# Expert weights in two buffer sets, gate columns computed in the feed-forward, and the residual's transposes inside expert 0

## The chip, the cores and the metric

The kernel runs on one core of a Trainium2 chip. The metric is the device time of one execution in microseconds (us), the median of several runs. PE is the matrix engine (PEld its weight loads), DVE the vector engine, ACT the scalar engine, POOL the GpSimd engine, and SP the engine whose queue starts most of the large DMA transfers.

## The reference

Two layers work on 512 latent tokens of width 1024 (and 256 context tokens). Each layer is an RMS norm with modulation, a projection into three token mixers (gated DeltaNet, attention, short convolution), an output projection, a gated residual, a second modulated norm and a channel mixer. In layer 0 the channel mixer is a dense feed-forward of width 2816, in layer 1 a mixture of 8 experts, of which each token uses two. The part that matters here is layer 1 from the output projection on:

```python
m_lat = (s_lat @ w_mod[l] + b_mod[l])[:, None, :]
sh1, sc1, g1, sh2, sc2, g2 = jnp.split(m_lat, 6, axis=-1)
...
x = x + g1 * out_l                              # out_l = cat @ w_out
hl2 = modulate(rmsnorm(x, norm2[l]), sh2, sc2)
x = x + g2 * channel_mixer(hl2, ...)            # layer 1: moe_swiglu
...
probs = jax.nn.softmax((h @ router).astype(F32), axis=-1)
top_p, top_i = lax.top_k(probs, TOP_K)
...
out = out + comb[..., e:e + 1] * swiglu(h, wg[e], wu[e], wd[e])
```

All is float32 at the ends. The gate row g2 of layer 1 stands in columns 5120 to 6143 of `s_lat @ w_mod[1]`, that is in column groups 10 and 11 of 512 columns each.

## The kernel before

**Weights.** Every weight tile is 128 x 1024 float32 (512 KB). `weight` loads it into a `raw` buffer through SP's queue (L196), ACT rounds it to `hi` (L207), and DVE subtracts to `lo` (L208); a product is then three matmuls (hi by hi, hi by lo, lo by hi). The pools that hold raw, hi and lo are opened by `weights`, and each tile waits until its buffer is free.

**Order of the work.** The program is written once as straight code, and a scheduler puts each engine's instructions into that engine's own order, by dependences and by when it takes each of them to be ready. Each engine then runs its row in order, so an instruction that waits holds up all behind it. DMA transfers stand in the row of the engine that issues them.

**The output projection of layer 1** (`tail`). The 512 tokens go in two pieces of 256: MID (token tiles 1 and 2) and ENDS (tiles 0 and 3). For each piece and each of eight blocks `m` of 128 output rows there is one `wout` tile and 24 matmuls (L215 to L217) over the eight parts `cat0` to `cat7`; then DVE adds to the residual tile `xr` in place (L730), which ACT's queue has loaded (L700). Raw has 4 buffers there, hi and lo 3. Just ahead, the last scan steps of gated DeltaNet and the last attention tiles run on the same engines (copies `L` and `a_pt` on ACT; `oacc` and `go_r` on DVE are the scan's output and its norm; `cat0` and `cat1` come from them last).

**The second norm.** After each piece, `stats` squares the eight blocks on ACT and DVE in turn, sums them in PE (L341), transposes the sums, takes the reciprocal root on DVE in 12 small steps (`rsq`, L239 to L246), and spreads it by a diagonal tile (`dg`) and a matmul (L357). DVE scales (L739) and ACT adds the shift (L740) to give `hh`. After the second piece, `mod_rows` computes the gate row: 8 `wmod` tiles, 32 matmuls (L265), a copy, a matmul with `sel` (L746) and an addition to `g2row` (L747).

**The mixture of experts** (`moe`). Router matmuls (L898), `lt` copies, four small transposes (L1062), scores `lg` (L1066). `route` picks two experts a token and computes each row's place: `sel`, four running sums `cum` (L1084), matmuls (L1087 to L1089), `pos`, `p0`, the one-hot `eq` (L1096), and from it the row numbers `first` of expert 0's tokens (L1102). The tokens of `hh` are transposed into `tk` (`tokens`) and written to memory by SP (L903); POOL gathers expert 0's rows `xa` and `xb` from there (L1227, L1235), PE transposes them, ACT and DVE split them into `xh` and `xl`. Then the residual `xr` is transposed into `tk` (32 transposes, L231 and L889), the pools of `hh` and `xr` are closed, and raw becomes a pool of 7 buffers in place of 4.

**The experts** (`Expert.run`). Each of the eight has ten steps: five of four gate and up tiles (`wmg`), one of two, and four of down tiles (`wmd`). Step `i` computes while the tiles of step `i+1` are loaded and split. hi and lo have 8 buffers each. Where an expert has more than 128 tokens, extra matmuls stand in a branch on a flag, which every engine reads out of `jobs` (L933, the branches L1267). `gate` and `out` (L1303, L1304) follow each step's matmuls; `gm` is the gated product. `Combine` gathers and adds the results during the last two experts.

## Time and profile before

| | us |
|---|---|
| median of 3 runs | 2132.27 (2132.15 to 2135.34) |
| the profiled execution | 2134.24 |
| its span, first to last instruction | 2132.5 |
| PE busy in the span | 2011.8 (94%) |
| DVE / ACT busy | 1398.4 / 996.0 |
| last matmul of layer 1's output projection starts | at 1499.67 |
| gather of expert 0's rows is issued | at 1528.44 |
| first matmul of expert 0 | at 1542.38 |

The profiled execution took 2.0 us longer than the median of the timed runs and 1.7 us longer than its own span. Times "at" are counted from the start of the span. PE is the engine to follow: stretches in which it is not busy, or in which its granted clock (PEclk, as a share of full speed) is below 1.00, are where time is lost.

### The profile page before, as it was taken

The numbers are of one execution on the slowest core, as the hardware profiler recorded it, in microseconds if no ns is written. First come the engines' busy times: TensorE is split into PE (matmuls) and PEld (weight loads), VectorE is DVE, ScalarE is ACT, GpSimd is POOL, SyncE is SP. The second block draws the span as 40 slices with busy tenths as digits, with TensorE's granted clock in tenths as the row PEclk, the third lists the DMA queues.
The fourth block names the chain that finished last, engine by engine and source line by source line (L and its number), as shares of the span: only waits on it lengthen the run. The fifth ranks groups of instructions, "written<-read, shape, count | busy, mean of one in ns | idle before, by whom it ended". The sixth has DMA issues, their size and how long they took to land. (4 is left out here: it accounts for less than half of the span.)

```text
span 2132.5 us, 33501 instructions
## 1 busy us (share of the span) xinstructions
PE 2011.8 (94%) x12422; PEld 1647.2 (77%) x12422; DVE 1398.4 (66%) x2501; ACT 996.0 (47%) x1748; POOL 229.5 (11%) x276
## 2 busy tenths in 40 slices
PE   6999899989999999999989998999789999999996
PEld 2998766768788888888879886778567777777774
DVE  3858855765896734242367598677576788666777
ACT  3665375543322222222246556654365576645555
POOL 0000222214000000000040004210110000000011
PEclk9999999999999999999999999999899999999998
DMA  6342543152564715131233333034597799667674
GB/s 260 93 134 70 166 163 115 33 172 93 197 207 129 246 42 206 33 102 50 69 123 108 102 102 117 22 117 146 168 327 255 257 353 332 214 222 240 241 277 157
DMA packets 123489, 344.56 MB, mean 162 GB/s; under 512 B 13280, under 2 KB 36816, under 8 KB 123312
## 3 DMA queue, kind: packets, MB, share of 16 engines
q1 hardware_dynamic: 81216, 273.85, 38.3%
q0 software_dynamic: 14608, 47.87, 6.7%
q10 hardware_dynamic: 27488, 20.52, 3.1%
q8 instruction: 106, 1.74, 0.3%
q14 instruction: 71, 0.58, 0.1%
HBM read 306.00 MB, written 36.19 MB: 160 GB/s over the span
## 5 line engine op out<-in xcount | busy, mean ns | idle before, releaser
L207 ACT ACTIVATE hi<-raw 128x1024 fp32r<-128x1024 f32 (+3 forms) x444 | 426.2, 987 | 302.2 <-PE ps L216 230.7
L208 DVE TENSOR_TENSOR lo<-raw,hi 128x1024 fp32r<-128x1024 f32 (+2 forms) x432 | 482.7, 1138 | 85.5 <-ACT hi L207 69.5
L215 PE MATMUL ps<-hh,hi 128*128 128x512 f32 (+1 forms) x1040 | 355.8, 342 | 0.8 <-ACT hi L207 0.8
L217 PE MATMUL ps<-hh,lo 128*128 128x512 f32 (+1 forms) x1040 | 353.9, 340 | 1.7 <-DVE lo L208 1.7
L216 PE MATMUL ps<-hl,hi 128*128 128x512 f32 (+1 forms) x1040 | 354.6, 341 | 0.0
L215 PEld LDWEIGHTS ps<-hh,hi 128*128 128x128 f32 x1040 | 198.2, 191 | 26.7 <-ACT hi L207 3.4
L217 PEld LDWEIGHTS ps<-hh,lo 128*128 128x128 f32 x1040 | 198.1, 190 | 24.2 <-DVE lo L208 2.5
L216 PEld LDWEIGHTS ps<-hl,hi 128*128 128x128 f32 x1040 | 198.3, 191 | 21.2
L223 PE MATMUL ps<-lo,xh 128*128 128x512 f32 (+1 forms) x384 | 150.6, 393 | 10.7 <-DVE lo L208 5.1
L221 PE MATMUL ps<-hi,xh 128*128 128x512 f32 (+1 forms) x384 | 145.9, 380 | 2.0 <-ACT hi L207 1.9
L222 PE MATMUL ps<-hi,xl 128*128 128x512 f32 (+1 forms) x384 | 144.7, 377 | 0.0
L1332 DVE TENSOR_TENSOR sg<-sg,ps 128x512 f32<-128x512 f32 (+1 forms) x44 | 24.4, 554 | 150.7 <-PE ps L217 150.7
L217 PE MATMUL ps<-gh,lo 128*128 128x256 f32 (+1 forms) x352 | 119.2, 338 | 2.8 <-DVE lo L208 2.8
L216 PE MATMUL ps<-gl,hi 128*128 128x256 f32 (+1 forms) x352 | 120.2, 342 | 0.0
L215 PE MATMUL ps<-gh,hi 128*128 128x256 f32 (+1 forms) x352 | 119.2, 339 | 0.0
L223 PEld LDWEIGHTS ps<-lo,xh 128*128 128x128 f32 x384 | 72.4, 189 | 38.7 <-DVE lo L208 16.5
L296 DVE SCALAR_TENSOR_TENSOR macc<-mraw,sT,macc 128x512 f32<-128x512 f32 x126 | 89.4, 749 | 13.7 <-DMA mraw<-wmod 12.8
L221 PE MATMUL ps<-hi,hh 128*128 128x400 f32 (+2 forms) x272 | 91.7, 338 | 1.3 <-ACT hi L207 1.1
L223 PE MATMUL ps<-lo,hh 128*128 128x400 f32 (+2 forms) x272 | 89.3, 330 | 0.6 <-DVE lo L208 0.6
L222 PE MATMUL ps<-hi,hl 128*128 128x400 f32 (+2 forms) x272 | 88.4, 326 | 0.0
L1574 DVE TENSOR_REDUCE a_st<-S 128x1 f32<-128x768 f32 (+1 forms) x80 | 66.2, 844 | 31.2 <-PE S L1573 30.8
L1575 ACT ACTIVATE a_p<-S,a_st 128x768 f32<-128x768 f32 (+1 forms) x80 | 65.1, 816 | 43.3 <-DVE a_st L1574 38.9
(594 smaller groups left out, 4140.4 us busy)
## 6 DMA issues: line engine op xcount, KB each, us to landing
raw<-wmg SPq DMA_DIRECT2D x176, 512.0 KB
raw<-wmd SPq DMA_DIRECT2D x80, 512.0 KB
raw<-wmod SPq DMA_DIRECT2D x48, 512.0 KB
mraw<-wmod SPq DMA_DIRECT2D x48, 512.0 KB
raw<-wgu SPq DMA_DIRECT2D x44, 512.0 KB
raw<-wout SPq DMA_DIRECT2D x32, 512.0 KB
raw<-wt SPq DMA_DIRECT2D x24, 512.0 KB
raw<-wd SPq DMA_DIRECT2D x32, 256.0 KB
```

The lines of the kernel that those rows point to most:

```text
L207: self.nc.scalar.activation(hi, src, AF.Copy)
L208: (eng or self.nc.vector).tensor_sub(lo, src, hi.bitcast(F32))
L215: mm(out, wh, xh, start=start, stop=False)
L216: mm(out, wh, xl, start=False, stop=False)
L217: mm(out, wl, xh, start=False, stop=stop)
L221: mm(out, xh, wh, start=start, stop=False)
L222: mm(out, xl, wh, start=False, stop=False)
L223: mm(out, xh, wl, start=False, stop=stop)
L296: nc.vector.scalar_tensor_tensor(a, w, c, a, op0=OP.mult, op1=OP.add)
L1332: nc.vector.tensor_mul(s, s, pu)
L1574: nc.vector.tensor_reduce(st[:, 0, c + i:c + i + 1], s[:, :n], axis=AX.X, op=OP.min)
L1575: nc.scalar.activation(P[:, :n], s[:, :n], AF.Exp, bias=st[:, 0, c + i:c + i + 1], scale=-1.0, accum_out=st[:, 1, c + i:c + i + 1])
```

## The change

1. **Two sets of buffers for the experts' tiles.** The even steps' set (raw 2, hi and lo 4 each) is opened before the pools of `hh` and `xr`, so that its tiles can be loaded and split during the output projection. The odd steps' set (raw 3, hi and lo 4 each) is opened in `moe`. At step 4 of expert 0 a common raw pool of 6 takes the place of both raw pools. Before, there was one set: hi and lo 8, raw 4 and then 7.
2. **The gate row.** Groups 10 and 11 of layer 1 join the twelve groups that `mod_acc` sums on DVE during layer 0's feed-forward (8 more `wmod` tiles, 16 more DVE operations of 128 x 512). `mod_row`, called behind f = 14 of 22, adds over the partitions with two matmuls, adds the bias and writes the row to memory; `tail` reads it back spread over 128 partitions. The 8 loads, the 32 matmuls and what follows them at the end of `tail` are gone.
3. **The norm.** In place of `stats`, layer 1 uses what layer 0 uses: `square` on ACT after each block with the sum on POOL, and `rms`: four small matmuls, the 12 steps, the diagonal and one matmul.
4. **Routing.** The `cum` additions become five matmuls into one sum; `p0` is read out of PSUM, and one operation less leads to `eq`. The tokens of `hh` are transposed in two halves, MID early and ENDS behind the scores; ACT's queue writes them in the order 1, 2, 0, 3. The gather of expert 0's rows is written ahead of the rest of the routing.
5. **The residual.** The 32 transposes of `xr`, the closing of its pools and the opening of `Combine` move to a hook at step 4 of expert 0; the load of the last norm's row moves there too, on SP's queue.

```diff
@@ new in the class Core
+    def mod_row(self, accs, b="ps"):
+        nc, mp = self.nc, self.mpool
+        p = self.psum(b)
+        for i, (*_, a) in enumerate(accs):
+            nc.tensor.matmul(p[32 * i:32 * i + 32, :512], self.C("ones")[:, :32], a, start=True, stop=True,
+                             tile_position=(0, 32 * i))
+        m = mp.tile([128, 512], F32, name="m")
+        for i, (l, g, *_, a) in enumerate(accs):
+            r = slice(32 * i, 32 * i + 1)
+            nc.scalar.dma_start(a[r], self.A["bmod"][l, 4 * g:4 * g + 4].rearrange("(o t) p -> o (t p)", o=1))
+            nc.vector.tensor_add(m[r], p[r, :512], a[r])
+            nc.scalar.dma_start(self.gate[(g - 10) * 512:(g - 9) * 512].rearrange("(o n) -> o n", o=1), m[r])
...
@@ tail
+    if last:
+        k.weights(e0, 4, pb, 2)
+        even = k.wraw, k.whl
     hp = pb(eh, "hp2")
...
-        nc.scalar.dma_start(g2row, bass.AP(tensor=A["bmod"].tensor, offset=A["bmod"].offset + (48 + 40) * 128, ap=[[0, 128], [1, 1024]]))
+        nc.scalar.dma_start(g2row, k.gate.partition_broadcast(128))
...
-                if not last:
-                    k.square(np_, acc, xm, m)
+                k.square(np_, acc, xm, m)
...
             elif last:
-                rs, = k.stats(np_, x, [(o, n)])
+                rs = k.rms(np_, acc, n, "pn")
...
-        if last:
-            sel = np_.tile([128, 128], F32, name="sel", bufs=1)
-            nc.vector.tensor_copy(sel, k.C("fold8")[:, 0:1].to_broadcast([128, 128]))
-            for h in range(2):
-                g, r, p = g2row[:, h * 512:h * 512 + 512], k.mod_rows(l, 10 + h, "ps"), k.psum()
-                nc.tensor.matmul(p, sel, r, start=True, stop=True)
-                nc.vector.tensor_add(g, g, p)
...
@@ ffn
-            for i, g in ((0, 10), (0, 11), (1, 2), (1, 3), (1, 0), (1, 1), (1, 4), (1, 5), (1, 6), (1, 7), (1, 8), (1, 9)):
+            for i, g in ((0, 10), (0, 11), (1, 2), (1, 3), (1, 0), (1, 1), (1, 4), (1, 5), (1, 6), (1, 7), (1, 8), (1, 9),
+                         (1, 10), (1, 11)):
...
+                elif f == 14:
+                    k.mod_row(done, "pn")
...
@@ moe
-        k.weights(es, 8, pa, 4)
-        ex = Expert(k, pa(es, "ex"))
+        k.weights(es, 4, pa, 3)
+        ex = Expert(k, pa(es, "ex"), (even, (k.wraw, k.whl)))
+        ex.first = [ex.load((0, 0, None), 0)]
...
+            tokens(hs, False, range(4)[MID])
...
-            tokens(hs, False)
-            for t in range(4):
-                nc.sync.dma_start(k.ht[t * 128:t * 128 + 128], tk[:, t])
             routing = route(k, hp, lt, slots, pw, jobs, first, last)
-            found = next(routing)
-            placed = next(routing)
+            with tc.issue_after(next(routing).ins):
+                tokens(hs, False, range(4)[ENDS])
+            for t in (1, 2, 0, 3):
+                nc.scalar.dma_start(k.ht[t * 128:t * 128 + 128], tk[:, t])
+            next(routing)
+            ex.idx = [(first[:, 0:1], first[:TAIL, 1:2])]
+            ex.prep(0, 0, True)
+
+            with tc.issue_after(next(routing).ins):
+                ex.first.append(ex.load((0, 0, None), 1))
+                ex.clear()
...
-        with tc.issue_after(found.ins):
-            ex.first = ex.load((0, 0, None), 0)
-        with tc.issue_after(placed.ins):
+        def residual():
+
             tokens(x, True)
-        close()
-        e2 = ExitStack()
-        pb = pools(k, l)[1]
-        k.weights(e2, None, pb, 7)
-        cb = Combine(k, pb(e2, "cb"), ex, tk, slots, pw, nfrow)
+            close()
+            k.weights(e2, None, pb, 6)
+            ex.sets = [(k.wraw, w) for _, w in ex.sets]
+            cb.append(Combine(k, pb(e2, "cb"), ex, tk, slots, pw))
+
...
+               {(0, 4): residual, (6, 1): lambda: cb[0].gathers(0), (6, 8): lambda: cb[0].others(0), (7, 1): lambda: cb[0].gathers(1),
...
@@ route
-    nc.vector.memset(cum[:, 0], 0.0)
+    p = k.psum()
+
+    nc.tensor.matmul(p[:, 0:32], k.C("stri"), sel.rearrange("p t e -> p (t e)"), start=True, stop=False, skip_group_check=True)
     for t in range(4):
-        nc.vector.tensor_add(cum[:, t + 1], cum[:, t], sel[:, t])
-    fl = lambda a: a.rearrange("p t e -> p (t e)")
-    p = k.psum()
-    nc.tensor.matmul(p[:, 0:32], k.C("stri"), fl(sel), start=True, stop=False)
-    nc.tensor.matmul(p[:, 0:32], k.C("ones"), fl(cum[:, 0:4]), start=False, stop=True)
-    nc.tensor.matmul(p[:, 32:40], k.C("ones"), cum[:, 4], start=True, stop=True)
+        nc.tensor.matmul(p[:, 8 * t + 8:40], k.C("ones"), sel[:, t:t + 1, :].to_broadcast([128, 4 - t, 8]), start=False, stop=t == 3,
+                         skip_group_check=True)
...
@@ class Expert
+        pre, self.first = self.first, []
+        load = lambda i: pre.pop(0) if pre else self.load(*work[i])
...
+        k.wraw, k.whl = self.sets[c % 2]
```

**Where instructions stand before and after.** ACT just ahead of the projection, before; `a_rs`, `W` and `a_pt` belong to the mixers, `xr` are the residual's loads:

```order
L700 DMA xr_13940<-xres 128x512
L700 DMA xr_13942<-xres 128x512
L700 DMA xr_13944<-xres 128x512
L1552 ACTIVATE a_rs<-t 128x256
L1888 ACTIVATE W<-pg 128x256
L700 DMA xr_13946<-xres 128x512
L1888 ACTIVATE W<-pg 128x256
L207 ACTIVATE cat6h<-a_pt 128x512
L1531 COPY a_pt<-t 128x512
L207 ACTIVATE cat7h<-a_pt 128x512
L1531 COPY a_pt<-t 128x512
L700 DMA xr_13948<-xres 128x512
```

ACT at the start of the projection after the change; of the three `hi` one is wout's and two are wmg's, and the four `cat0h` and `cat1h` are the scan's last output:

```order
L209 ACTIVATE cat5h<-a_y 128x512
L209 ACTIVATE hi<-raw 128x1024 x3
L209 ACTIVATE cat0h<-pg 128x2x64
L719 DMA xr_13994<-xres 128x512
L209 ACTIVATE cat0h<-pg 128x2x64
L719 DMA xr_13996<-xres 128x512
L209 ACTIVATE cat1h<-pg 128x2x64
L719 DMA xr_13998<-xres 128x512
L209 ACTIVATE cat1h<-pg 128x2x64
L719 DMA xr_14000<-xres 128x512
L719 DMA xr_14002<-xres 128x512
L719 DMA xr_14004<-xres 128x512
```

The residual's loads have moved from between the mixers' operations to behind the scan's last output. DVE at the start of the projection, before; `lo_13986`, `lo_14018` and `lo_14050` are the first three wout tiles, `oacc` in the eleventh row the scan's output with its norm applied, and `rquo` and `rqio` the steps to that norm:

```order
L208 TENSOR_TENSOR cat5l_12152<-a_y_13103,cat5h_12151 128x512
L245 SCALAR_TENSOR_TENSOR rquo_13819<-rquo_13819,rqxo_13818 128x8
L208 TENSOR_TENSOR lo_13986<-raw_13983,hi_13985 128x1024
L246 SCALAR_TENSOR_TENSOR rqio_13820<-rquo_13819,rqio_13820 128x8
L208 TENSOR_TENSOR lo_14018<-raw_14015,hi_14017 128x1024
L244 TENSOR_TENSOR rquo_13819<-rqio_13820 128x8
L208 TENSOR_TENSOR lo_14050<-raw_14047,hi_14049 128x1024
L245 SCALAR_TENSOR_TENSOR rquo_13819<-rquo_13819,rqxo_13818 128x8
L743 COPY sel_14629<-cst_67 128x128
L246 SCALAR_TENSOR_TENSOR go_r_13816<-rquo_13819,rqio_13820 128x8
L1958 TENSOR_TENSOR oacc_12858<-oacc_12858,go_r_13816 128x2x256
L730 SCALAR_TENSOR_TENSOR xr0_13940<-ps_13989,modc1_75,xr0_13940 128x256
```

DVE at the same place after; `lo_14710` and `lo_14716` are wmg tiles of step 0, `lo_14042`, `lo_14075` and `lo_14110` the first three wout tiles:

```order
L210 TENSOR_TENSOR lo_14710<-raw_14707,hi_14709 128x1024
L246 TENSOR_TENSOR rquo_13864<-rqio_13865 128x8
L210 TENSOR_TENSOR cat5l_12197<-a_y_13148,cat5h_12196 128x512
L247 SCALAR_TENSOR_TENSOR rquo_13864<-rquo_13864,rqxo_13863 128x8
L210 TENSOR_TENSOR lo_14716<-raw_14713,hi_14715 128x1024
L248 SCALAR_TENSOR_TENSOR rqio_13865<-rquo_13864,rqio_13865 128x8
L210 TENSOR_TENSOR lo_14042<-raw_14039,hi_14041 128x1024
L246 TENSOR_TENSOR rquo_13864<-rqio_13865 128x8
L210 TENSOR_TENSOR lo_14075<-raw_14072,hi_14074 128x1024
L247 SCALAR_TENSOR_TENSOR rquo_13864<-rquo_13864,rqxo_13863 128x8
L210 TENSOR_TENSOR lo_14110<-raw_14107,hi_14109 128x1024
L248 SCALAR_TENSOR_TENSOR rqio_13865<-rquo_13864,rqio_13865 128x8
```

Two subtractions for expert tiles now stand ahead of the first wout tile's; behind these rows come two more (`lo_14722`, `lo_14728`) ahead of the row that applies the norm to `oacc`. PE at the end of the routing, before; `eq` gives the row numbers, `xr` is the residual:

```order
L1101 MATMUL ps<-cst,eq 128x1 x4
L1101 MATMUL ps<-cst,eq 64x1 x4
L231 MATMUL pt<-cst,xr_13940 128x128
L231 MATMUL pt<-cst,xr_13942 128x128
L231 MATMUL pt<-cst,xr_13944 128x128
L231 MATMUL pt<-cst,xr_13946 128x128
L231 MATMUL pt<-cst,xr_13948 128x128
L231 MATMUL pt<-cst,xr_13950 128x128
```

PE at the same place after, and then PE at the start of step 4 of expert 0 after; `xa` and `xb` are the gathered rows, `hi`, `lo` the expert's tiles:

```order
L1125 MATMUL ps<-cst,eq 128x1 x4
L1125 MATMUL ps<-cst,eq 64x1 x4
L233 MATMUL pt<-cst,xa 128x128 x8
L223 MATMUL ps<-hi,xh 128x512 x2
L233 MATMUL pt<-cst,xb 128x64 x8
L224 MATMUL ps<-hi,xl 128x512
L225 MATMUL ps<-lo,xh 128x512
L223 MATMUL ps<-hi,xh 128x512
```

```order
L233 MATMUL pt<-cst,xr_13994 128x128
L233 MATMUL pt<-cst,xr_13996 128x128
L233 MATMUL pt<-cst,xr_13998 128x128
L233 MATMUL pt<-cst,xr_14000 128x128
L223 MATMUL ps<-hi,xh 128x512
L224 MATMUL ps<-hi,xl 128x512
L225 MATMUL ps<-lo,xh 128x512
L223 MATMUL ps<-hi,xh 128x512
L233 MATMUL pt<-cst,xr_14002 128x128
L233 MATMUL pt<-cst,xr_14004 128x128
```

Between the row numbers and the gathered rows nothing is left for PE; the residual's transposes now stand in groups of four and eight between the matmuls of step 4. SP from the last loads of the mixers to expert 0, before; `ex` is the tokens written to memory:

```order
L196 DMA raw<-wt 128x1024 x7
L196 DMA raw<-wout 128x1024 x16
L196 DMA raw<-wmod 128x1024 x4
L196 DMA raw<-wmg 128x1024
L196 DMA raw<-wmod 128x1024 x4
L196 DMA raw<-wmg 128x1024 x3
L903 DMA ex_80<-tk 128x1024 x4
L933 TENSOR_LOAD jobs
L933 ISA x2
```

SP at the same place after:

```order
L198 DMA raw<-wt 128x1024 x7
L198 DMA raw<-wmg 128x1024 x2
L198 DMA raw<-wout 128x1024 x4
L198 DMA raw<-wmg 128x1024 x2
L198 DMA raw<-wout 128x1024 x3
L198 DMA raw<-wmg 128x1024 x2
L198 DMA raw<-wout 128x1024 x9
L198 DMA raw<-wmg 128x1024 x3
L955 TENSOR_LOAD jobs
L955 ISA x2
L198 DMA raw<-wmg 128x1024 x4
```

Before, four expert tiles are issued ahead of the read of `jobs`, at which SP waits for the routing; after, nine are.

## Rows read from the trace of the kernel before

**Rows 1.** The page: span, instructions, busy time of each engine.

```profile
span 2132.5 us, 33501 instructions
...
PE 2011.8 (94%) x12422; PEld 1647.2 (77%) x12422; DVE 1398.4 (66%) x2501; ACT 996.0 (47%) x1748; POOL 229.5 (11%) x276
```

**Rows 2.** Stretches: length, busy time (instructions) by engine, PEclk, DMA share, GB/s.

```profile
700.00:760.00 60.00, 60.00 (x334) 52.55 (x335) 41.13 (x66) 11.00 (x15) 0.00 (x0) 1.00 0.64 215
...
1530.00:1540.00 10.00, 4.30 (x20) 3.34 (x19) 8.02 (x34) 0.93 (x2) 3.89 (x5) 0.51 0.44 131
1540.00:1550.00 10.00, 7.55 (x40) 5.24 (x39) 3.69 (x6) 3.72 (x7) 4.85 (x5) 1.00 0.81 94
1540.00:1600.00 60.00, 52.47 (x245) 38.30 (x244) 42.66 (x50) 39.80 (x52) 11.90 (x12) 1.00 0.98 297
1700.00:1800.00 100.00, 96.37 (x446) 73.64 (x445) 88.44 (x100) 73.86 (x95) 7.21 (x10) 1.00 0.97 351
```

**Rows 3.** ACT's timeline ahead of the projection: start, length, instruction.

```profile
1418.07 0.82 ACTq L700 DMA_DIRECT2D xr<-xres  x2
...
1452.56 0.28 ACT L207 ACTIVATE cat0h<-pg 128x128 fp32r<-128x128 f32 x1
```

**Rows 4.** DVE's timeline in the projection; in brackets the idle time before.

```profile
1445.06 1.22 DVE L208 TENSOR_TENSOR lo<-raw,hi 128x1024 fp32r<-128x1024 f32 x1
...
1449.02 0.69 DVE L1958 TENSOR_TENSOR oacc<-oacc,go_r 128x512 f32<-128x512 f32 x1
...
1471.39 0.48 DVE L730 SCALAR_TENSOR_TENSOR xr<-ps,modc,xr 128x256 f32<-128x256 f32 x1 [0.68 <-PE ps L217]
...
1478.70 0.48 DVE L730 SCALAR_TENSOR_TENSOR xr<-ps,modc,xr 128x256 f32<-128x256 f32 x1 [2.20 <-PE ps L217]
```

**Rows 5.** PE's timeline from the last projection matmul to expert 0.

```profile
1499.67 0.28 PE L217 MATMUL ps<-cat5h,lo 128*128 128x256 f32 x1
...
1509.33 0.67 PE L357 MATMUL pn<-dg,cst 128*128 128x256 f32 x2 [1.19 <-DVE dg L352]
...
1513.83 2.81 PE L898 MATMUL ps<-hh,router 128*32 128x256 f32 x32
...
1536.62 4.33 PE L231 MATMUL pt<-cst,xr 128*128 128x128 f32 x20 [5.70 <-DVE tk L889]
1541.04 1.28 PE L231 MATMUL pt<-cst,xa 128*128 128x128 f32 x8
1542.38 0.50 PE L221 MATMUL ps<-hi,xh 128*128 128x512 f32 x1
```

**Rows 6.** DVE's timeline through the second norm, the scores and the routing.

```profile
1506.38 0.17 DVE L239 TENSOR_SCALAR rqxs<-ss 128x2 f32<-128x2 f32 x1
...
1510.04 3.22 DVE L739 SCALAR_TENSOR_TENSOR hh<-xr,gain,pn 128x256 f32<-128x256 f32 x8 [0.85 <-PE pn L357]
...
1518.49 0.19 DVE L1066 COPY lg<-ps 128x32 f32<-128x32 f32 x1 [1.39 <-PE ps L1062]
...
1521.41 0.17 DVE L1084 TENSOR_TENSOR cum<-cum,sel 128x8 f32<-128x8 f32 x1
...
1527.23 0.16 DVE L1102 CAST first<-ps 128x1 int32<-128x1 f32 x1 [2.53 <-PE ps L1101]
```

**Rows 7.** POOL's timeline: the gather of expert 0's rows.

```profile
1528.44 1.38 POOL L1227 DMA_INDIRECT xa<-ex,first  x1 [101.11 <-DVE ex L1118]
```

**Rows 8.** What touches xa, 1520 to 1570; least, median, most.

```profile
L231 PEld LDWEIGHTS pt<-cst,xa x8: 138/140/143, 1541.0 to 1541.9; 128*128 128x128 f32 x8
...
DMA to landing us min/median/max: 4.7/4.7/4.7
```

**Rows 9.** Groups of PE, 600 to 760: count, busy us, mean ns.

```profile
L306 PE MATMUL pn<-macc,cst 128*32 128x512 f32 x16 | 2.1, 604 | 0.0
```

**Rows 10.** Groups of ACT, 1540 to 1600; behind the bar idle time before, releasers.

```profile
L207 ACT ACTIVATE hi<-raw 128x1024 fp32r<-128x1024 f32 (+1 forms) x31 | 31.3, 1029 | 10.6 <-DMA raw<-wmg 9.6 <-DMA raw<-wmd 0.7
```

**Rows 11.** Groups of DVE, 1700 to 1800.

```profile
L208 DVE TENSOR_TENSOR lo<-raw,hi 128x1024 fp32r<-128x1024 f32 x64 | 74.3, 1188 | 6.8 <-ACTq L1267 4.2 <-ACT hi L207 1.8 <-DVEq L1267 0.5
```

More of the change, by code (lines that the diff above doesn't have):

```diff
@@ L721, in tail @@
         for s, o, n in pieces:
-            acc = None if last else k.acc if s else [np_.tile([128, 512], F32, name=f"nac{i}", bufs=1) for i in range(2)]
+            acc = k.acc if s else [np_.tile([128, 512], F32, name=f"nac{i}")[:, :n] for i in range(2)]
             for m in range(8):
@@ L883, in moe, with tokens @@
         nc.vector.tensor_copy(tid, k.C("tokid"))
-        def tokens(src, dve):
-            for t in range(4):
+        def tokens(src, dve, ts=range(4)):
+            for t in ts:
                 for q in range(2):
```

72 lines of the change are left out of this document (38 added, 34 removed).

## The prediction

> **What bounds the kernel now.** I read the page first: PE is busy for 2011.8 of 2132.5 us [rows 1], so only about 120 us of the span can be won without removing matmuls. The table of stretches then shows where they lie. In the feed-forward (700 to 760) PE is busy for 60.00 of 60 us while DVE has 41 of 60. [...] From 1540 to 1600, expert 0, it is busy for 52.47 of 60, and from 1700 to 1800, in later experts, for 96.37 of 100 with DMA engines at 0.97 and DVE at 88.44 [rows 2]. [...]
>
> [...] The last projection matmul starts at 1499.67 and takes 0.28 [rows 5]; call its end, 1499.95, E. The first scaling of the second norm runs at 1510.04, the scores are copied at 1518.49, the row numbers are cast at 1527.23 [rows 6], POOL issues the gather at 1528.44 [rows 7], which lands 4.7 us later [rows 8], at 1533.1. Yet PE starts on the gathered rows only at 1541.04, behind 20 residual transposes that began at 1536.62 after 5.70 us of waiting for DVE's copies, and the first matmul of expert 0 comes at 1542.38 [rows 5]. That is 42.4 us from E.
>
> **The change part by part.** Times are against the profiled execution.
>
> *Head of the projection.* As the order shows, DVE does two subtractions for expert tiles ahead of the first wout tile's. Each takes 1.22 us, and the first wout one started at 1445.06 [rows 4]: +2.4 for PE, which waits for it. Two more stand ahead of the operation that applies the norm to the scan's output (1449.02 [rows 4]), so the last `cat0h` and `cat1h`, of which the first ran at 1452.56 [rows 3], come at about 1457. The residual's loads, issued from 1418.07 on before [rows 3], now stand behind these on ACT; and behind the loads stand the squares of the first three blocks and only then the `hi` of the fifth wout tile. With some 3 us for such a load (the gather, with its indices, needs 4.7 [rows 8]) that `hi` comes at about 1462 where PE would want its block: I put another 2.1 on this. Together +4.5. Lower end +1.5 (ACT and DVE have the expert tiles ready early); upper end +8, if the residual's eight loads and the gate row (2.6 MB) take their 7.5 us at 351 GB/s [rows 2] in front of PE.
>
> *First piece's norm.* The residual additions of consecutive blocks stand 2.88 us apart in the projection, but 7.31 where the first `stats` falls into PE's row (1471.39 to 1478.70 [rows 4]). The 4.4 us go; the small matmuls of `rms` cost some 0.4: −4.0 (−4.4 to −3).
>
> *Second piece's norm.* From E to the first scaling it is 10.1 us. After: addition and square 0.5 each, as long as a residual addition of that size [rows 4], four small matmuls 0.75 (0.14 for each weight load [rows 8] and the last one's way through), then from the first of the 12 steps (1506.38) to the first scaling 3.66 as now [rows 6], in all 5.4: −4.7. The gate row leaves this chain as well; that only makes the 3.66 safer.
>
> *Scaling to scores.* The router's matmuls ended at 1516.64 [rows 5], 6.6 us behind the first scaling, though the eight scalings take 3.22 [rows 6]; the gate row's copy, matmul and addition sat among them. Without these I give the last shift and its matmuls 0.9 behind the scalings: −2.5 (−2.9 to −1).
>
> *Routing.* Four running sums of 0.17, some 0.2 apart [rows 6], and two small steps of the same kind ahead of `eq` go; a fifth matmul comes: −1.3 (−1.8 to 0).
>
> *Gather to first matmul.* 13.9 us now. After: landing 4.7, then 1.34 from the first transpose to the first matmul (1541.04 to 1542.38 [rows 5]), and 0.8 because PE will be cold: 6.8, so −7.1 (−7.9 to −6). Nothing of the residual is ahead any more. But DVE has three subtractions of step 1 (1.22 each) and two clears ahead of `xl`, where before it did the step 0 ones during the routing: +1 (0 to +3).
>
> The first matmul of expert 0 thus moves by 4.5 − 4.0 − 4.7 − 2.5 − 1.3 − 7.1 = −15.1, its continuation by −14.1.
>
> *Cold start.* With no transposes in the wait, PE does nothing between the row numbers and the gathered rows. Today 20 transposes take 4.33 us at the half clock and 8 after them 1.28 [rows 5], and from 1540 the granted clock is 1.00 [rows 2]; so after a wait like this about 4 us run at half speed. Then those were transposes, now it is step 0: +2 (0 to +2.2). [...] If the clock stayed up through the wait, the sum would be lower by these 2 us.
>
> *Residual inside expert 0.* 32 transposes at 0.14 each, the spacing of their weight loads (140 ns [rows 8]): +4.5 on PE (4 to 4.8). DVE copies four of 0.69, 2.8 us, into a step in which it is already busy for 88% [rows 2]; what does not fit makes weights late: +1.5 (0 to +2.8).
>
> *Expert 0's waits.* PE loses 7.5 of 60 us in 1540 to 1600, against 2.2 per 60 at the rate of 1700 to 1800 [rows 2], and ACT stood idle for 9.6 us for gate and up tiles to arrive [rows 10]. Nine tiles instead of four are issued before SP stops at `jobs`, so at the start of expert 0 all of step 1 and half of step 2 are in place. Of the excess of 5.4 I take −4.5 (−5.4 to 0).
>
> *Buffers later.* hi and lo are 4 + 4 instead of a ring of 8, raw 6 instead of 7. The trace shows nothing like it: below, nothing; above, one tile's transfer (512 KB at 351 GB/s, 1.5 us [rows 2]) lost once in each of four of the later experts, 6. DVE's subtractions there wait for ACT's `hi` for only 1.8 us in 100 [rows 11], which is near the lower end: +1.
>
> *Feed-forward.* 16 operations on DVE and 8 tiles of DMA traffic lie under a PE that is fully busy, with DVE at 41 and DMA at 0.64 of its time [rows 2]. If that cover were missing, 16 operations, each of half the columns of a 1.22 us subtraction [rows 4], would be some 10 us. Two matmuls of 0.60 like those of `mod_sum` [rows 9], side by side: +0.5 (0 to 1.2).
>
> Sum: −14.1 + 2 + 4.5 + 1.5 − 4.5 + 1 + 0.5 = −9.1. The profiled execution took 2134.24, 2.0 above the median, as one of three shown did by 3; taken from the median, 2132.27 − 9.1 gives **2123** us.
>
> **The rivals.**
>
> *The waits in expert 0 vanish whole.* The head costs only its 1.5 and the copies and buffers nothing: −9.1 − 3 − 1.5 − 1 − 0.9 = −15.5, 2117. For it: SP is stopped for less long and nine tiles are ahead. Against it: DMA engines are at 0.98 over 1540 to 1600 [rows 2], so whatever is prefetched must still be refilled.
>
> *The head eats the gain.* ACT's queue, with the residual's loads and their waits, holds up wout's `hi` block after block, +8 instead of +4.5, and the late start of `jobs` and tiles leaves expert 0 with its waits (−1 instead of −4.5): −2.1, 2130. For it: the loads move by some 35 us and lose all their slack. Against it: six projection sums can stand in PSUM, so additions may be late without PE waiting; only the `hi` matters.
>
> *The experts pay (slower).* Two sets of 4 bind a tile to its step's parity, so that a tile of step i+2 cannot be split before step i's matmuls are through with the buffer; where steps have two or three tiles, a ring of 8 would be ahead. It decides from the point at which the seven later experts lose more than (9.1 + 4.3 + 1) / 7 = 2.1 us each; at 3 us each the kernel would take 2132.3 − 9.1 − 1 + 21 = 2143. For it: PE loses only 3.6 us in 100 there, with DVE at 88% and DMA at 0.97 [rows 2], so little is needed. Against it: a step's tiles are at most four, and half of 8 buffers is what the ring could be ahead anyway.
>
> *Nothing of it reaches the end.* If expert 0 is bound by the transfers alone, an earlier start of PE only becomes waiting: the stream of tiles resumes when SP gets `jobs`, some 14 us earlier by the same chain, so this holds only if `jobs` comes no earlier. About 2131.
>
> **How the numbers follow.** The forecast (−5 to −13) has 0.56, the larger gain 0.15, the eaten head 0.13, the experts' price 0.08, nothing 0.08. A run of this kernel tells 0.2%, 4.3 us, from no change. Faster: 0.56 + 0.15 + a part of the head's case, 0.04, and some of the price's where it is small, 0.03, in all 0.78. Same: 0.15. Slower: 0.07. The range: with every term at its good end the sum is about −22, with every one at its bad end +8; I leave out the outermost of both and take 2113 to 2132.
>
> **What would show it.** Right: the additions of consecutive blocks 2.9 us apart throughout; first scaling about 5.4 us behind the last projection matmul; first matmul of expert 0 near 1527, at a low clock; tokens gathered with no transposes between; PE idle less than 4 us in expert 0; residual transposes, some 4.5 us in sum, in step 4. Wrong: a wait for `hi` or `lo` in the first six blocks of more than 5 us; expert 0 taking as long as now from its first to last step though transfers are ahead; steps of later experts longer than before by more than 0.2 us each.

## The result

The change takes 2147.08 us (median of 4 runs, 2146.63 to 2151.04) against 2132.21 for the kernel before: a ratio of 1.0075, 95% interval 1.0054 to 1.0095. It is slower by some 15 us by the medians (16 by the ratio) where 9 us faster was forecast, and lies outside the range.

### The profile after

The page: span, and busy time of each engine as in [rows 1].

```profile
span 2145.1 us, 33436 instructions
...
PE 2006.3 (94%) x12374; PEld 1650.2 (77%) x12374; DVE 1405.4 (66%) x2500; ACT 998.7 (47%) x1752; POOL 246.2 (11%) x288
```

PE has 5.5 us less to do than in [rows 1] and the span is 12.6 longer, so the loss is not more work: it is waiting, and matmuls at a lower granted clock (0.975 in the mean of the span against 0.980). DVE's timeline, the operations that mark the stages: the eighth residual addition and the ninth (the first piece's norm lies between), the sixteenth, the first scaling of the second norm, the scores, the row numbers, and of expert 0 the products of the fifth and sixth steps and the second of the two `y`.

```profile
1480.39 0.48 DVE L749 SCALAR_TENSOR_TENSOR xr<-ps,modc,xr 128x256 f32<-128x256 f32 x1 [0.63 <-PE ps L219]
1484.46 0.48 DVE L749 SCALAR_TENSOR_TENSOR xr<-ps,modc,xr 128x256 f32<-128x256 f32 x1 [0.58 <-PE ps L219]
...
1505.40 0.48 DVE L749 SCALAR_TENSOR_TENSOR xr<-ps,modc,xr 128x256 f32<-128x256 f32 x1 [2.39 <-PE ps L219]
...
1510.83 3.22 DVE L757 SCALAR_TENSOR_TENSOR hh<-xr,gain,pn 128x256 f32<-128x256 f32 x8 [0.79 <-PE pn L407]
1517.93 0.19 DVE L1093 COPY lg<-ps 128x32 f32<-128x32 f32 x1 [0.82 <-PE ps L1088]
1526.24 0.16 DVE L1126 CAST first<-ps 128x1 int32<-128x1 f32 x1 [2.59 <-PE ps L1125]
...
1581.89 0.41 DVE L1334 TENSOR_TENSOR gm<-gm,ps 128x256 f32<-128x256 f32 x1
1598.78 0.28 DVE L1334 TENSOR_TENSOR gm<-gm,ps 128x128 f32<-128x128 f32 x1
...
1610.49 0.69 DVE L1352 TENSOR_TENSOR y<-ps,g2row 128x512 f32<-128x512 f32 x1 [1.33 <-PE ps L225]
```

PE's timeline: where it waits in the projection, the gathered rows, and a stretch of steps 3 and 4 with the first residual transposes.

```profile
1465.04 0.58 PE L217 MATMUL ps<-cat6h,hi 128*128 128x256 f32 x1 [3.42 <-ACT hi L209]
...
1471.34 0.41 PE L217 MATMUL ps<-cat6h,hi 128*128 128x256 f32 x1
1471.55 0.41 PE L218 MATMUL ps<-cat6l,hi 128*128 128x256 f32 x1
...
1531.31 1.94 PE L233 MATMUL pt<-cst,xa 128*128 128x128 f32 x8 [5.11 <-DMA xa<-ex,first]
1536.79 1.11 PE L233 MATMUL pt<-cst,xb 64*128 64x64 f32 x8 [2.42 <-DVE xl L210]
...
1561.14 1.04 PE L233 MATMUL pt<-cst,gm 128*128 128x128 f32 x2 [3.28 <-DVEq L1297]
1561.83 0.78 PE L223 MATMUL ps<-hi,xh 128*128 128x512 f32 x1
...
1566.67 0.63 PE L225 MATMUL ps<-lo,xh 128*128 128x512 f32 x1
1567.10 0.54 PE L223 MATMUL ps<-hi,xh 128*128 128x512 f32 x1
1567.48 0.39 PE L224 MATMUL ps<-hi,xl 128*128 128x512 f32 x1
1567.70 0.39 PE L225 MATMUL ps<-lo,xh 128*128 128x512 f32 x1
...
1571.09 0.63 PE L233 MATMUL pt<-cst,xr 128*128 128x128 f32 x4
```

Stretches, columns as in [rows 2]:

```profile
1450.00:1460.00 10.00, 9.41 (x74) 9.21 (x73) 5.79 (x16) 3.23 (x6) 0.00 (x0) 0.93 0.97 356
1460.00:1470.00 10.00, 5.94 (x32) 5.44 (x31) 6.35 (x8) 5.22 (x8) 3.03 (x3) 0.75 0.84 292
...
1530.00:1540.00 10.00, 6.27 (x23) 4.78 (x24) 8.30 (x21) 2.63 (x4) 6.87 (x5) 0.50 0.77 166
1540.00:1550.00 10.00, 9.85 (x36) 7.38 (x36) 3.84 (x8) 3.67 (x4) 3.42 (x5) 0.82 0.77 105
1550.00:1560.00 10.00, 7.70 (x34) 5.55 (x32) 5.62 (x6) 5.62 (x7) 3.57 (x4) 1.00 0.64 197
1560.00:1570.00 10.00, 8.71 (x26) 6.64 (x26) 5.08 (x7) 4.56 (x6) 0.00 (x0) 0.66 0.61 179
1570.00:1580.00 10.00, 9.55 (x58) 7.64 (x58) 5.76 (x10) 3.97 (x7) 0.00 (x0) 1.00 0.26 84
1580.00:1590.00 10.00, 5.80 (x24) 4.47 (x23) 5.98 (x7) 5.28 (x7) 0.00 (x0) 0.72 1.00 379
```

In expert 0 the DMA share drops to 0.26 between 1570 and 1580, and PE has too little work in the ten microseconds behind that, when the share is 1.00. Before, the share over 1540 to 1600 was 0.98 [rows 2]. Two of the waits of SP's row over 1500 to 1600 (us in total, times, longest) and its timeline say why:

```profile
SPq L198 <- DVE lo L210: 29.5, 13, 5.4
...
SPq L976 <- PE pt L233: 7.7, 1, 7.7
```

```profile
1505.39 64.79 SPq L198 DMA_DIRECT2D raw<-wmg  x14
1578.02 0.33 SPq L976 DMA_DIRECT2D nfrow<-normf  x1
1578.40 1.07 SPq L198 DMA_DIRECT2D raw<-wmg  x2
```

SP stood for 7.7 us at the load of the last norm's row, until the last residual transposes were through; gate and up tiles stood behind it. The wait of 3.28 us at 1561 has another origin, which ACT's and DVE's timelines show:

```profile
1552.53 1.06 ACT L209 ACTIVATE hi<-raw 128x1024 fp32r<-128x1024 f32 x1 [5.82 <-DMA raw<-wmg]
...
1558.31 2.35 DVE L210 TENSOR_TENSOR lo<-raw,hi 128x1024 fp32r<-128x1024 f32 x2
1560.58 0.41 DVE L1334 TENSOR_TENSOR gm<-gm,ps 128x256 f32<-128x256 f32 x1
```

ACT stood idle for a tile, its `hi` came late, and the product that PE wanted stood in DVE's row behind the subtractions for late tiles.

Cutting the profiled executions at the same operations gives the sum of the whole change (us; each cell is the difference of two starts; "last `cat5l`" is the split that ends just ahead of the projection, "second y" the later `y` of expert 0; e2, e4 and e9 are experiments below):

| stretch | before | change | forecast of the difference | e2 | e4 | e9 |
|---|---|---|---|---|---|---|
| start to last `cat5l` | 1444.4 | 1444.6 | +0.5 | 1451.0 | 1443.1 | 1441.6 |
| to the 16th addition | 55.6 | 60.8 | +4.5 − 4.0 | 58.4 | 52.4 | 51.5 |
| to the row numbers | 27.2 | 20.8 | −8.5 | 20.4 | 20.4 | 18.7 |
| to expert 0's first matmul | 15.2 | 6.9 | −7.1 | 6.9 | 7.0 | 7.0 |
| to its second y | 61.7 | 77.3 | +4.5 | 67.8 | 69.5 | 61.6 |
| to the last norm's `cs` | 515.8 | 521.7 | +1.0 | 520.7 | 515.1 | 516.2 |
| to the end | 12.7 | 13.0 | 0 | 13.2 | 12.8 | 13.1 |
| span | 2132.5 | 2145.1 | −9.1 | 2138.3 | 2120.3 | 2109.7 |

Ahead of the projection executions of like code differ by several us (first row), so experiments are read from the stretches behind it as well as from their times. The forecast's gains are there (−14.7 in rows three and four against −15.6). Three losses outweigh them: +5.2 in the projection, +15.7 in expert 0, +5.9 in the later experts.

### The profile page after: what moved, and what is told of

It is laid out like the page before. It is cut to its first block, busy times and chain, and to the rows that moved or that the text cites. A ratio compares the mean times of both kernels' runs of the same rounds, so it can differ in the third digit from the quotient of the medians.

```text
span 2145.1 us, 33436 instructions
## 1 busy us (share of the span) xinstructions
PE 2006.3 (94%) x12374; PEld 1650.2 (77%) x12374; DVE 1405.4 (66%) x2500; ACT 998.7 (47%) x1752; POOL 246.2 (11%) x288
## 5 line engine op out<-in xcount | busy, mean ns | idle before, releaser
L298 DVE SCALAR_TENSOR_TENSOR macc<-mraw,sT,macc 128x512 f32<-128x512 f32 x140 | 99.6, 746 | 19.2 <-DMA mraw<-wmod 18.5
L224 PEld LDWEIGHTS ps<-hi,xl 128*128 128x128 f32 x384 | 75.0, 195 | 16.2 <-issue 1.4
L223 PEld LDWEIGHTS ps<-hi,xh 128*128 128x128 f32 x384 | 75.1, 196 | 15.7 <-ACT hi L209 2.8
```

The lines of the kernel that those rows point to most:

```text
L223: mm(out, xh, wh, start=start, stop=False)
L224: mm(out, xl, wh, start=False, stop=False)
L298: nc.vector.scalar_tensor_tensor(a, w, c, a, op0=OP.mult, op1=OP.add)
```

## Experiments

In all of the expectations "first y" means the second y of the table, as their figures show. Every ratio is to the kernel before, run beside it.

**e1.** The load of the last norm's row goes through POOL's queue.

```diff
-        k.nc.sync.dma_start(self.nfrow, k.A["normf"].rearrange("o n -> (o n)").partition_broadcast(128))
+        k.nc.gpsimd.dma_start(self.nfrow, k.A["normf"].rearrange("o n -> (o n)").partition_broadcast(128))
```

> The changed kernel, with one line altered: the last norm's row, loaded at step 4 of expert 0, is issued from POOL's row in place of SP's. SP waited 7.7 us at this load for PE, and the first gate product behind it came 6.2 us later than before, where the one ahead of it came 0.6 us earlier. Theory A (that load alone holds SP's row, and the weight tiles behind it): the sixth gate product of expert 0 some 6 us earlier, in all 2141 against 2147. Theory B (the common raw pool opened there lies in the same memory and waits for the same transposes, so the tiles behind it wait as well): no more than 1 us gained, 2146.

2145.33, ratio 1.0067 (1.0043 to 1.0091). From the fifth to the sixth product it takes 13.98 us where the change takes 16.89 and the kernel before 10.03. So 2.9 of the 6.9 came from this load alone; the rest stays: the common raw pool lies in the memory that `hh` and `xr` give up, and SP's row now shows 8.5 us of waiting for the same transposes at a tile. This is read from the trace; the time itself is not told apart from the change's.

**e2.** The residual is written ahead of the experts instead of inside step 4 of expert 0.

```diff
+        residual()
         flags = nc.values_load(jobs[0:1, 8:9], min_val=0, max_val=256 * NJOBS + 255)
-               {(0, 4): residual, (6, 1): lambda: cb[0].gathers(0), ...
+               {(6, 1): lambda: cb[0].gathers(0), ...
```

> The changed kernel, with the residual's transposes, the closing of its pools, the common raw pool and the last norm's row moved back ahead of expert 0. Theory A (expert 0 is slow because its tiles have only 2 and 3 raw buffers up to step 4, in one SP row, and because of the wait at step 4): PE can do the transposes while it waits for the gathered rows, raw is 6 deep from the start, expert 0 from its first to its last product takes about as long as before (50 us against 64 now), in all 2147 - 12 = 2135. Theory B (the transposes and copies cost their 4.5 to 6 us of PE and DVE time wherever they stand, nothing else): expert 0 gets shorter by 5 and starts later by as much, 2147.

2137.04, ratio 1.0023 (1.0010 to 1.0036): 10 us faster than the change. Expert 0 takes 67.8 us to its second y, 9.5 less. The transposes then run from 1544.0 to 1550.8, and SP waits for them at the same load, now for longer,

```profile
SPq L977 <- PE pt L233: 14.1, 1, 14.1
```

but early, with nine tiles in hand; the fifth to sixth product takes 9.91. The time is 2 us above theory A's. Part 5's place inside step 4, with the common raw pool that opens behind it, was thus worth some 10 us of loss.

**e3.** Step 0's tiles are loaded and split only behind the last block of the first piece, in the same buffers.

```diff
+                if last and o == MID and m == 7:
+                    k.late = list(k.at)
...
+            for i in k.late:
+                el.enter_context(tc.issue_after(i.ins))
+            ex.first = [ex.load((0, 0, None), 0)]
```

(`k.at` holds the last load and the last split.)

> The changed kernel, with the four loads, roundings and subtractions of expert 0's step 0 held behind the last block's of the projection's first piece. Now the eighth block's residual addition of the first piece comes 9.0 us later than before (1480.4 against 1471.4). Theory A (the residual's loads are late because of where their buffers lie, and hold ACT's row): it stays 6 us late or more, as those loads do not move, in all 2144 to 2147. Theory B (DVE's and ACT's work on the expert tiles at the head of the projection delays it): it comes within 2 us of before, in all 2139 to 2141.

2146.19, ratio 1.0070 (1.0048 to 1.0092). DVE's part of the head is gone (PE's first wait for a `lo` is 2.14, in the change 3.75), but the residual still comes late:

```profile
1455.18 1.67 ACTq L719 DMA_DIRECT2D xr<-xres  x2
...
1466.36 0.42 ACT L391 ACTIVATE nac<-xr 128x256 f32<-128x256 f32 x1 [7.21 <-DMA xr<-xres]
```

This is ACT's timeline; before, the loads were issued from 1418.07 on [rows 3]. The tiles' splits are not what moved them: theory A. The profiled execution was the longest of the four, 2155.75, and its projection takes 64.7 us from the last `cat5l` to the 16th addition, more than the change's 60.8; two of the held tiles are issued at 1456.25, beside the residual's loads.

**e4.** Parts 2 to 4 alone: one set of eight hi and lo buffers, raw 4 and then 7, the residual written ahead of the experts, and the last norm's row loaded early through ACT's queue, as before.

```diff
-    if last:
-        k.weights(e0, 4, pb, 2)
-        even = k.wraw, k.whl
...
-        k.weights(es, 4, pa, 3)
-        ex = Expert(k, pa(es, "ex"), (even, (k.wraw, k.whl)))
-        ex.first = [ex.load((0, 0, None), 0)]
+        k.weights(es, 8, pa, 4)
+        ex = Expert(k, pa(es, "ex"), ((k.wraw, k.whl),) * 2)
...
-            k.weights(e2, None, pb, 6)
+            k.weights(e2, None, pb, 7)
```

> Parts 2 to 4 of the change alone: gate row in the feed-forward, the norm by sums on POOL, the routing; one set of buffers as before (hi and lo 8, raw 4 and then 7), the residual and the last norm's row ahead of expert 0 as before. Theory A (all the loss lies in parts 1 and 5): the projection ends some 4 us earlier than before, the scores come 9 to 11 us earlier, and with the residual's transposes again ahead of the gathered rows part of it is kept, 2132 - 8 = 2124. Theory B (what these parts win only becomes waiting at expert 0 for weight tiles): 2132.

2119.56, ratio 0.9945 (0.9927 to 0.9963): faster than both, and 4 us below theory A's time. The residual's loads stand early again, and the later experts take 515.1 us as before. Expert 0 loses 7.9 us, though; two of its stretches:

```profile
1520.00:1530.00 10.00, 6.12 (x25) 4.90 (x26) 8.67 (x23) 1.79 (x3) 6.94 (x6) 0.50 0.29 77
1530.00:1540.00 10.00, 9.29 (x48) 6.80 (x47) 3.31 (x9) 4.00 (x7) 3.31 (x4) 0.87 0.27 14
```

DMA moves 14 GB/s there while the residual's transposes are done, and SP's row shows a wait for them of 16.8 us: the raw pool of 7 waits for the memory under `xr`, now in step 0.

**e5.** All steps use the odd set; the even set is named but no tile is taken from it.

```diff
-        ex = Expert(k, pa(es, "ex"), (even, (k.wraw, k.whl)))
+        ex = Expert(k, pa(es, "ex"), ((k.wraw, k.whl),) * 2)
```

> The changed kernel, in which the even steps' set is opened as before but never used: all steps take the odd steps' buffers, so no expert tile is loaded, rounded or subtracted during the projection. Only the projection is read from this run (the experts have half the buffers and will be slow). Theory A (the set's memory pushes the residual's tiles onto buffers that the mixers still use, their loads come late and hold ACT's row): the residual's loads stand behind the scan's last output, the first residual addition comes some 9 us later than with parts 2 to 4 alone (1459 against 1450.1) and the eighth of the first piece as well (about 1479 against 1470.5). Theory B (the expert tiles' own work at the head delays it): both within 2 us of parts 2 to 4 alone.

2208.25 in one run; its experts, with one small set, are not read. The residual's loads are back at 1418.28 and the eighth addition at 1471.53, as before. It does not tell memory from tiles: a pool from which nothing is taken seems to occupy nothing, so both were gone. e11 mends that.

**e6 and e7.** e4 with one size changed: a raw pool of 6, and hi and lo in two sets of 4.

```diff
-            k.weights(e2, None, pb, 7)
+            k.weights(e2, None, pb, 6)
```

```diff
-        k.weights(es, 8, pa, 4)
-        ex = Expert(k, pa(es, "ex"), ((k.wraw, k.whl),) * 2)
+        k.weights(es, 4, pa, 4)
+        even = k.whl
+        k.whl = [pa(es, "v" + x, 4) for x in "hl"]
+        ex = Expert(k, pa(es, "ex"), ((k.wraw, even), (k.wraw, k.whl)))
```

> Parts 2 to 4 alone, with the raw pool of the experts 6 deep in place of 7. Theory A (the changed kernel loses its 6 us between the end of expert 0 and the end through the raw pool's missing buffer): the stretch from expert 0's second output to the final norm is 520 us or more in place of 515.1, in all 2119.6 + 5 = 2125. Theory B (through the two sets of hi and lo): 515 to 517, in all 2120 to 2121.

> Parts 2 to 4 alone, with hi and lo in two sets of 4 by the step's parity in place of one ring of 8, raw as in the kernel before (4, then 7). Theory A (the raw pool's missing buffer costs the later experts): the same as parts 2 to 4 alone, 2119.6, and 515 us from expert 0's second output to the final norm. Theory B (the sets): 519 us or more there, in all 2123 to 2125.

e6: 2126.51, ratio 0.9970 (0.9956 to 0.9984). From the second y to `cs` 520.1 us against 515.1 in e4: +0.9 and +1.9 in experts 2 and 3, +2.0 in the last, counted from y to y. e7: 2125.68, ratio 0.9960 (0.9940 to 0.9979), 520.7 us, nearly all of it in the last expert. In the four traces with one set of eight and seven raw buffers (before, e4, e8, e9) this stretch is 515.1 to 516.2, so both sizes show in it; by its time alone e7 is not told apart from e4. DVE's timeline of e7 and PE's waits over 2060 to 2130 there:

```profile
2093.91 0.75 DVE L1030 SCALAR_TENSOR_TENSOR y<-ps,cw,g2row 128x512 f32<-128x512 f32 x1
2101.59 0.74 DVE L1030 SCALAR_TENSOR_TENSOR y<-ps,cw,g2row 128x512 f32<-128x512 f32 x1
```

```profile
PE ps L1035 <- ACT xl L209: 2.3, 1, 2.3
```

The last expert's two `y` are 7.7 us apart, as in the change; before and in e4 they are 2.8 apart, and this wait isn't among PE's. Both sizes cost, in different experts; together in the change they cost 5.9, less than the 10.6 that the two sum to.

**e8.** e4 with eight tiles instead of four issued ahead of `jobs`.

```diff
-                ex.first.append(ex.load((0, 0, None), 0))
+                ex.first += [ex.load((0, 0, None), c) for c in range(2)]
...
+        with tc.issue_after(loaded.ins):
+            flags = nc.values_load(jobs[0:1, 8:9], min_val=0, max_val=256 * NJOBS + 255)
```

> Parts 2 to 4 alone, with the four tiles of step 1 also issued ahead of the read of jobs in SP's row (eight tiles in place of four, through the same 4 raw buffers). Expert 0 from its first matmul to its second output takes 69.5 us with parts 2 to 4 alone against 61.7 before. Theory A (it waits for tiles that are issued late): 63 to 65 us, in all 2119.6 - 5 = 2114 to 2115. Theory B (it waits for the transfers' rate, or for the gathers and scatters that share the DMA engines): 68 us or more, in all 2118 to 2120.

2124.94, ratio 0.9958 (0.9944 to 0.9973). From the gather to the second y 76.1 us, as in e4, which is theory B; the time is 5 us above its figure, and why was not pursued. The four added tiles stand ahead of `jobs`, but SP waits 26.2 us for a raw buffer first and issues them from 1524.78 on, 6.1 us behind the gather. The pool behind them is held up as in e4 (17.0 us for the transposes).

**e9.** e4 with the 32 residual transposes on PE around the row numbers (eight ahead of the matmuls with `eq`, 24 behind), so that they run while the gather is awaited, and their copies on ACT.

```diff
+            placed = next(routing)
+            with tc.issue_after(placed.ins):
+                tokens(x, False)
             ex.idx = [(first[:, 0:1], first[:TAIL, 1:2])]
             ex.prep(0, 0, True)
...
-            tokens(x, True)
             close()
```

> The kernel of e4 (gate columns, norm beside the scaling, routing as in the change; one set of eight hi and lo buffers, seven raw ones), with the residual's 32 transposes on TensorE directly ahead of expert 0's, so that they run while the gather is awaited, and their copies all on ACT. Theory A: what is left in the stretch from gather to the first y of expert 0 (76.1 us in e4 and e8, with DMA idle at about .27 while the raw pool's memory waits for the residual's transposes) is that wait; with it gone the stretch takes 68 us or less (e2 had 74.3 with them ahead but only six raw buffers in two rows) and the time falls to some 2112. Theory B: the stretch is bound by the rate at which 5 MB of weights land; it stays at 74 to 76 us and the time at 2118 to 2121, as e4.

2117.50 (2111.23 to 2119.34), ratio 0.9928 (0.9909 to 0.9947). From the gather to the second y 67.7 us: theory A in the trace. Its time of 2112 is met by the profiled execution alone, the fastest of six; the median is not told apart from e4's by these intervals. Two stretches, and two rows of PE:

```profile
1520.00:1530.00 10.00, 6.89 (x23) 5.13 (x24) 8.88 (x20) 4.72 (x5) 7.77 (x7) 0.66 1.13 282
1530.00:1540.00 10.00, 9.85 (x44) 7.72 (x43) 3.92 (x4) 4.22 (x5) 0.00 (x0) 1.00 0.97 134
...
1518.79 0.50 PE L223 MATMUL ps<-hi,xh 128*128 128x512 f32 x1 [0.25 <-ACT xh L209]
1522.96 1.11 PE L233 MATMUL pt<-cst,xb 64*128 64x64 f32 x8 [3.67 <-DVE xl L210]
```

The DMA engines no longer pause (share 1.13 and 0.97, in e4 0.29 and 0.27): SP's wait for the transposes, 16.8 us in e4, is 1.1. The clock was not spared: expert 0's first matmul takes 0.50 us, in e4 0.79, but PE then waits 3.67 us for `xl`, and the granted clock from 1520 to 1530 is 0.66.

**e10.** e9 with e8's eight tiles.

> The kernel of e9 with eight tiles of expert 0's weights loaded, split and kept ahead of the routing's row numbers (as e8). Theory A of e9: with the memory free early, loads that are issued earlier land earlier, and the stretch from gather to the first y falls by another 0 to 3 us, time 2109 to 2113. Theory B: no different from e9, within 2 us.

2128.04, ratio 0.9970 (0.9953 to 0.9987): both theories missed. From the gather to the second y 75.3 us, as if e9's edit were undone, and 523.8 from there to `cs`. SP's waits over 1480 to 1600:

```profile
SPq L198 <- DVE lo L210: 56.1, 25, 29.0
```

SP stood for 29.0 us at one tile until a subtraction freed its buffer (in e8 26.2; in e9 it stood 21.1 at `jobs`). SP's timeline around the gather, in e9 (1510 to 1520), then in e10 (1515 to 1526):

```profile
1515.52 4.75 SPq L198 DMA_DIRECT2D raw<-wmg  x7
...
1520.88 4.98 SPq L198 DMA_DIRECT2D raw<-wmg  x5
```

The edit did not bring loads forward: counted from the gather (1512.74 and 1514.75), the fifth tile is issued after 2.8 us in e9 and after 6.1 in e10, because it waits for one of the 4 early buffers where e9 takes it from the pool of 7. SP reads `jobs` only behind the eight tiles, at 1524.67, where e9 reads it at 1514.53; the first tile of the pool of 7 then comes 10.8 us behind the gather, in e9 2.8. These 8.0 us are about what the stretch loses; no run tests it. Why the later experts lose another 8 us was not pursued.

**e11.** The change with the even set replaced by one tile of its 40 KB of a partition; all steps use the odd set.

```diff
-        k.weights(e0, 4, pb, 2)
-        even = k.wraw, k.whl
+        pad = pb(e0, "pad").tile([128, 10240], F32, name="pad")
+        nc.vector.memset(pad[:, 0:1], 0.0)
+        even = None
...
-        ex = Expert(k, pa(es, "ex"), (even, (k.wraw, k.whl)))
+        ex = Expert(k, pa(es, "ex"), ((k.wraw, k.whl),) * 2)
```

> The changed kernel with every step's hi and lo in the odd steps' four buffers, and the even set's place taken by one tile of the same 40 KB of a partition that is only cleared. No even tile is loaded or split during the projection. Only the projection is read from it. Theory A (the set's memory moves the residual tiles onto buffers that the mixers still use): the residual's loads start near 1455 and the eighth addition is 8 to 10 us later, measured from the last piece of attention rows, than in the kernel before. Theory B (it was the even tiles' loads and splits): the loads start near 1418 and the additions stand as before.

2208.39 in one run, of which only the projection is read. ACT's timeline:

```profile
1446.30 0.28 ACT L209 ACTIVATE cat0h<-pg 128x128 fp32r<-128x128 f32 x1 [0.40 <-PE pg L233]
1446.38 2.15 ACTq L720 DMA_DIRECT2D xr<-xres  x2
...
1453.35 0.42 ACT L391 ACTIVATE nac<-xr 128x256 f32<-128x256 f32 x1 [2.52 <-DMA xr<-xres]
```

The same row of ACT in the change, and the stretch of e11 that answers to 1460 to 1470 there:

```profile
1463.01 0.42 ACT L391 ACTIVATE nac<-xr 128x256 f32<-128x256 f32 x1 [5.76 <-DMA xr<-xres]
...
1450.00:1460.00 10.00, 7.13 (x57) 6.72 (x57) 6.62 (x10) 5.87 (x10) 3.03 (x3) 1.00 0.87 311
```

The memory alone moves the loads behind the first `cat0h`, as in the change: theory A as to the place. Its price was too high: the eighth addition, counted from the last `cat5l`, is 3.4 us later than before, not 8 to 10, and the projection, from the last `cat5l` to the 16th addition, takes 55.5 us, 3.0 more than e4's 52.4, not the 8.4 of the change. The other 5.4 are read from PE's rows. It idles 8.4 us in the change and 5.0 here. Of the 3.4 between, 1.6 are the first wait for a `lo` (3.75 against 2.14: DVE's subtractions for expert tiles), 1.5 the wait for the `hi` that stands behind the residual's loads (3.42 against 1.93). The remaining 2.0 are clock: behind the wait of 3.42 the granted clock from 1460 to 1470 is 0.75, here 1.00, and matmuls of 256 columns stand 0.21 us apart up to 1471.55 and 0.12 from 1471.92 on. That the residual lands later in the change (ACT waits 5.76 us for `xr`, here 2.52) because four `wmg` tiles are issued among wout's (DMA share 0.97 at 356 GB/s from 1450 to 1460) is likely, but no run isolates it.

## Why the prediction was wrong, step by step

**What held.** The first piece's norm: from the eighth to the ninth addition 4.07 us instead of 7.31 [rows 4], −3.2 (forecast −4.0). The second norm: 5.4 from the 16th addition to the first scaling, as forecast. Scaling to scores 7.1 (forecast 6.0); the granted clock of that stretch is 0.76, and in e9, where it is 1.00, the stretch takes 6.2. From the scores to the row numbers only 0.4 was won: 8.3 against 8.7 in [rows 6] (forecast 7.4). The matmuls that sum up the places end 4.2 us behind the scores before and after, so they took what the running sums gave back. In e9 it is 7.1, because the 16 matmuls with `eq` take 1.61 us there and 2.81 before and in the change. Gather to first matmul 6.5, as forecast to 0.3; the wait for `xl` 2.4 (forecast +1, at most 3): DVE has the three subtractions and two clears ahead of it, as the order said. e4 keeps these gains and is 0.55% faster than before; that is the test that parts 2 to 4 were right. The feed-forward's +0.5 cannot be read, since executions of like code differ by several us there.

**Head of the projection** was mis-sized: +4.5 forecast, about +8.4 measured (60.8 against e4's 52.4, both with the new norm). DVE's part, forecast at +2.4, was 1.8 (PE's first wait for a `lo`, 3.75 against e4's 1.98). ACT's part, forecast at +2.1, was the rest: 3.42 for the `hi`, 1.2 in two smaller waits, and 2.0 at the lower clock behind them (0.75 from 1460 to 1470), which the forecast did not price here. The order had shown that the loads move and the text saw ACT's row hold up `hi`. What I had not asked is why they move (the even set's memory pushes `xr` onto buffers that the mixers still use: e11; e3 shows it is not the splits) and what 0.5 MB tiles beside them may do to their landing: the forecast's some 3 us for such a load was an estimate, and the median to landing is 6.1 us in the change and 4.7 in e11. The upper end, +8, was of the right size.

**Expert 0's waits** is the step that failed in kind: −4.5 forecast from nine tiles ahead. The products of expert 0's steps, counted from its first matmul, came at 13.6, 27.4, 36.6, 40.7, 48.7 and 65.6 us, before at 11.5, 22.5, 28.6, 33.3, 40.2 and 50.2. So 8.0 is lost by the third step (2.1, 2.8 and 3.1 a step) and 6.9 between the fifth and sixth. PE's rows give the first 8.0 to three things: the lower clock at the start (under the cold start, below), the wait of 3.28 at 1561 behind a late tile, and the lower clock behind that wait. That tiles are late, though nine were ahead, is put down to small raw pools in one in-order row: even and odd tiles alternate in pools of 2 and 3, SP's row stops at each buffer that a subtraction has not freed (13 waits, 29.5 us; 5.4 the longest), and from 1530 to 1590 ACT stands idle for 14.6 us for gate and up tiles (9.6 in [rows 10], over the like 60 us). The nine tiles were used up and not replaced in time: the DMA share is 0.64 and 0.61 between 1550 and 1570, where 1540 to 1600 had 0.98 before. The sum of SP's waits alone does not show it: they all lie in 1530 to 1600, and over the like 70 us of the kernel before (1539 to 1609) it is 30.3 us in 19 waits. That raw pools are at fault in these steps was not tried alone; e2, which has the common pool of 6 from the start, loses 3.1 by the third step, with the transposes ahead of it.

**Residual inside expert 0** was costed at its work, +4.5 on PE and +1.5 on DVE. The work was less: in step 4 the 32 transposes add some 3.2 us to PE's row. The price was in what the step holds up, which the forecast left out, though the load on SP's queue stands in the change's fifth part: `nfrow` and the common raw pool wait for the transposes and every tile waits behind them. e1 recovers 2.9 of 6.9, e2 all of it.

**Cold start.** PE began expert 0 at a granted clock of 0.50 (1530 to 1540), after a wait of 5.1 us with nothing to do. It cost more than +2, about 2.9 by the rows above: half of the 2.2 us from 1537.8, where step 0's matmuls resume behind the wait for `xl`, to 1540, and 0.18 of the next ten, whose granted clock is 0.82; what PE lost ahead of that lies under the wait. The clock fell once more after the wait of 3.28 at 1561: from 1561.83 to 1566.67 matmuls stand 0.43 apart, from 1567.48 on 0.23, another 2.4 us (0.66 from 1560 to 1570); and again behind 1580, with 0.72 over ten us. So the lower clock was priced at one place and came at several, the projection among them.

With transposes in the wait (e9) expert 0's first matmul, at 1518.79, takes 0.50 us, where in the change and in e4 it takes 0.79, and the granted clock from 1510 to 1520 is 0.83. The lower clock then comes behind the wait of 3.67 us for `xl`: the matmuls from 1524.59 to 1526.72 stand 0.43 apart, from 1529.20 on 0.23.

**Buffers later** was mis-sized: +1 forecast, +5.9 measured, the bound of 6. Both sizes cost (e6, e7), and neither as the slower rival had it: a raw pool of 6 costs experts 2 and 3 and the last one to two us each, and the two sets cost the last alone, whose second y comes 7.7 instead of 2.8 behind the first (not traced further). That rival named 2143, nearest to what came, but from 3 us in each of seven experts; without these 5.9 the kernel would still be slower than before. What came is not its mechanism.

**The cover that was missing.** The forecast summed what each edit costs and took the DMA row of SP as free. The head (+8.4), expert 0 (+7.8 over e4) and the later experts (+6.6 over e4) make 22.8 of the 24.8 us between the spans of e4 and the change; 1.5 of the rest lies ahead of the projection, where executions differ anyway. The range was also narrower than its own terms: with every term at its bad end the sum is +13.3 and not +8 (8 − 3 − 4.7 − 1 − 6 + 3 + 2.2 + 4.8 + 2.8 + 6 + 1.2), which is 2145.6.

## What to carry to other kernels

When a pool is closed and another opened in the middle of a stream, ask which row issues the new pool's first load, and what its memory waits for; that wait is paid by every load behind it in that row (7.7 us here), not by the step alone. More buffers for one stage are memory taken from another: look in the order at where the displaced tiles' loads now stand (1418 to 1455 here) before costing the gain. Work that an engine can do in a wait (e9's transposes) is better put there than beside a stage that is already full, even if it looks free of dependences in both places; in the traces expert 0 takes 7.9 us less in e9 than in e4, though their medians are not told apart.
